# One hybrid decoder layer on one core: a norm row spread by products, a separate bank for the first sums, early small tables, and one query copy moved to VectorE

## The chip, the core and the metric

The kernel runs on one core of a Trainium2 chip. A core has TensorE (PE: matrix products; its weight loads are shown as PEld), VectorE (DVE), ScalarE (ACT), GpSimd (POOL) and SyncE (SP, which here only issues transfers), a two-dimensional on-chip memory of 128 rows, and a smaller accumulation memory of eight banks into which TensorE writes. Transfers between the chip's main memory and the on-chip memory are run by 16 DMA engines. They are issued from SP, ACT and POOL. The engines run side by side and wait for each other by semaphores; each takes its own instructions in the order of the program.

The metric is the device time of one execution in microseconds (us).

## The reference, cut to what matters

One layer is computed twice: for a prompt of 1024 tokens (8 tiles of 128) and for a sample step of 8 sequences of 8 tokens with 512 cached tokens each. Both begin with a root-mean-square norm and one combined projection of 3872 columns.

```python
def rms_norm(x, g):
    x32 = x.astype(jnp.float32)
    y = x32 * lax.rsqrt(jnp.mean(x32 * x32, axis=-1, keepdims=True) + EPS)
    return (y * g.astype(jnp.float32)).astype(x.dtype)
...
    h = rms_norm(x, g_norm)
    proj = jnp.einsum('btd,dn->btn', h, w_in)
    qa, kc, vc, ks, vs, kw, vw, ga, za, qb, kb, vb, fb, zb = jnp.split(proj, SPLIT_POINTS, axis=-1)
...
    # group A: sparse attention, three branches with gates
    return gates[..., 0:1] * o_c + gates[..., 1:2] * o_s + gates[..., 2:3] * o_w
    # group B (fox): softmax attention with a decaying bias
    s = s + (jnp.transpose(cq, (0, 2, 1))[:, :, :, None] - jnp.transpose(ck, (0, 2, 1))[:, :, None, :])
...
    u = jnp.concatenate([oa.reshape(B, T, -1) * jax.nn.silu(za), ob.reshape(B, T, -1) * jax.nn.silu(zb)], axis=-1)
    return x + jnp.einsum('btm,md->btd', u, w_out).astype(x.dtype)
```

At these sizes the prompt has 16 selection blocks and the reference takes the 16 best, so the selected branch is plain causal attention.

## The kernel before, in words

**Stages.** The projection runs over 15 chunks of at most 288 columns; chunk 0 holds keys and values of the compressed branch. Each chunk goes over 8 prompt tiles and one tile of sample tokens. Eleven chunks run first, with the cache's compression as background work; the last four are mixed with the attention of group B. Then comes the attention of group A, one tile of 128 queries after the other (`nsa_tile`), mixed in tiles 0 to 3 with the sample's attention (`sample_nsa`, `sample_fox`) and from tile 4 on with the output projection (`project_out`, and `project_last` for the last tile).

**Number format.** A float32 operand is split into a high and a low float16 part, and a product is three products: high by high, high by low, low by high. So a tile of x gives `xth` and `xtl`, a chunk of weights gives `wsp` with both parts, and attention probabilities give `phi` and `plo`.

**The start.** `first_loads` fetches the norm's weights g twice: as `g8`, 8 numbers to a row, from which a product with `ones` and a reduction make the common scale `gmax`, and as `gb`, the whole row of 1024 in each of the 128 rows, written by one broadcast transfer. `x_tile(0)` squares a tile on ScalarE (L163), makes its scale on POOL (L164, L165), multiplies x by scale and `gb` on VectorE (L166, tile `xsq`), turns it on TensorE (L171) and splits it on ScalarE (L176, `xth`) and VectorE (L177, `xtl`). `load_w` fetches a chunk's weights in four quarters (`wst`), squares them on ScalarE (L202), sums the squares with a product with `ones` (L205), reduces on VectorE (L206, L207), takes the power -0.5 on POOL (L208), and then scales and splits (L220, L216, L217 on ScalarE; L221 on VectorE; L218 on POOL). The products of the projection are L246. The sums of L205 and the transposes of L171 share the two banks named `tr`.

**Late in the program.** `nsa_queries(t)` fetches, scales and splits the queries of tile t, turns them on TensorE (L1076) and copies the result to `q1` on ScalarE (L1080); a transfer issued by ScalarE (L1081) copies its rows 64 to 127 to rows 0 to 63 of `qm` (`nqm` in the profile). The maxima of the scores (`nsa_max`, products L1103) need `qm`, and so do the scores (L1147).

**What sets the order.** The program is built with a scheduler that replays the written code against its own model of times and so fixes, engine by engine, the order in which the instructions stand. A change in one place can move instructions in places that it doesn't touch.

Of the kernel before, what the change touches and what calls it, by code (L numbers as in the profile page):

```python
# [11 lines left out]
F32 = mybir.dt.float32  # L12
# [4 lines left out]
AF = mybir.ActivationFunctionType  # L17
# [4 lines left out]
D = 1024  # L22
# [71 lines left out]
def layer_kernel(ctx, tc, a, o):  # L94
    nc = tc.nc
    P = ctx.enter_context(tc.tile_pool(name="const", bufs=1))
# [9 lines left out]
    ones = P.tile([128, 128], F32, name="ones")  # L106
    nhalf = P.tile([128, 32], F32, name="nhalf")
    block = P.tile([24, 512], F16, name="block")
    ident16 = P.tile([128, 128], F16, name="ident16")
    nsc = P.tile([128, 10], F32, name="nsc")  # L110
    wsc = P.tile([128, 16], F32, name="wsc")
    nc.vector.memset(nhalf, -0.5)
# [65 lines left out]

    bank = {"tr": ("ctr", 1), "acc": ("acc", 4, 288), "ws": 2}
    w_in = a["w_in"][0].rearrange("(kt p) n -> p kt n", p=128)  # L180

    def load_w(cols, vcols=None, vi=None, split=None):

# [10 lines left out]
        for q in range(4):  # L194
# [8 lines left out]
            st.append(s)  # L203
        p = PS.tile([128, 12], F32, name="tr", bufs=bank["ws"])
        nc.tensor.matmul(p[:, 0:used], ones, sv[:, 0:used], start=True, stop=True)  # L205
        nc.vector.tensor_reduce(out=sv[:, 12:13], in_=p[:, 0:used], axis=AX.X, op=ALU.add)  # L206
        nc.vector.tensor_scalar(sv[:, 13:14], sv[:, 12:13], 2.0 ** -30, TINY, op0=ALU.mult, op1=ALU.add)  # L207
# [668 lines left out]

    def load_chunk(ci):
        kind, cols, c = chunks[ci]
        vi = {"slc": 0, "win": 1, "vb": 2 + c}.get(kind)
        return load_w(cols, None if vi is None else slice(128, 256) if vi < 2 else slice(0, 256), vi,  # L880
                      True if kind == "z" else None)

# [32 lines left out]
    def first_loads():  # L915
        nc.scalar.dma_start(g8[:, 0], a["g_norm"][0].rearrange("(p k) -> p k", k=8))
        nc.scalar.dma_start(ident, a["c_ident"])
        nc.scalar.dma_start(gb, a["g_norm"].to_broadcast([128, D]))
        nc.vector.memset(ones, 1.0)
        nc.vector.tensor_tensor(g8[:, 1], g8[:, 0], g8[:, 0], op=ALU.mult)  # L920
        p = PS.tile([128, 512], F32, name="tr", bufs=2)
        nc.tensor.matmul(p[:, 0:8], ones, g8[:, 1], start=True, stop=True)
        nc.vector.tensor_reduce(out=gmax[:, 1:2], in_=p[:, 0:8], axis=AX.X, op=ALU.add)
        nc.vector.tensor_scalar(gmax[:, 0:1], gmax[:, 1:2], 2.0 ** -30, 1e-30, op0=ALU.mult, op1=ALU.max)
        nc.vector.tensor_scalar(gmax[:, 3:4], gmax[:, 0:1], D * EPS, None, op0=ALU.mult)

    def setup():
# [4 lines left out]
    def setup_loads():  # L932
        for i, n in enumerate(("gq_a", "gk_slc", "gk_win", "gq_b", "gk_b", "gk_cmp")):
            nc.sync.dma_start(grow[:, 64 * i:64 * i + 64], a[n])
        nc.sync.dma_start(grow[:, 384:392], a["b_f"])
        nc.sync.dma_start(block, a["c_block"])
        nc.sync.dma_start(ptab, a["page_table"].rearrange("(one b) j -> one (b j)", one=1))

# [11 lines left out]
    x_tile(0)  # L950
    setup()
    loaded = load_chunk(0)
    x_tile(1)
# [17 lines left out]
    PS = SP.enter_context(tc.tile_pool(name="ps2", bufs=1, space=PSUM, reuse_waits="tile"))  # L971
    bank.update({"smax": ("smax", 2), "tr": ("tr", 1), "acc": ("acc", 2, 512), "pv": ("pv", 1), "ws": 1})
    C2 = SC.enter_context(tc.tile_pool(name="fxc", bufs=1, reuse_waits="tile"))
# [93 lines left out]
    def nsa_queries(t):  # L1067
        q = BN.tile([128, 8, 64], F32, name="nq", bufs=1)
        nc.sync.dma_start(q.rearrange("p h d -> p (h d)"), qpark[t])
        qsp = BN.tile([128, 8, 128], F16, name="nqs", bufs=1)  # L1070
        split16(q, nsc[:, 1:2], qsp[:, :, 64:128], qsp[:, :, 0:64], nc.gpsimd if t else nc.vector)
        r = []
        for g in range(2):
            p = turned(t)
            for i in range(4):
                nc.tensor.transpose(p[:, i * 128:(i + 1) * 128], qsp[:, 4 * g + i], ident16)  # L1076
            q1 = BN.tile([128, 512], F16, name="nq1", bufs=4)
            qm = BN.tile([128, 512], F16, name="nqm", bufs=4)
            nc.gpsimd.memset(qm[64:88], 0.0)
            nc.scalar.activation(q1, p, AF.Copy)  # L1080
            nc.scalar.dma_start(qm[0:64], q1[64:128])  # L1081
            r.append((q1, qm))
        return r
# [136 lines left out]
    nc.gpsimd.dma_start(cnew, a["c_new"])  # L1220
    heado = C5.tile([128, 2], F32, name="heado")
    nc.sync.dma_start(heado, a["c_head"])
    spread = C5.tile([128, NB, 128], F32R, name="spread")
# [26 lines left out]
    def sample_decay():  # L1250
# [3 lines left out]
        l8 = B5.tile([64, NB, 8], F32, name="sl8", bufs=1)  # L1254
        bm = B5.tile([64, 8], F32, name="sbm", bufs=1)
        nc.sync.dma_start(bm, a["c_batch"][0:64])
        nc.vector.tensor_tensor(l8, bc(logf[0:64, 8:9], [64, NB, 8]), bc(bm[:, :, None], [64, NB, 8]), op=ALU.mult)
# [397 lines left out]
```

## Time and profile before

| | |
|---|---|
| three runs (us) | 973.31, 966.92, 971.30; median 971.3 |
| the profiled execution (us) | 971.47, of which the span of the core is 969.7 |
| granted TensorE clock, mean over the span | 0.979 |
| busy share of the span | PE 93%, PEld 70%, DVE 67%, ACT 66%, POOL 38% |

A row of the time line reads: start, duration, engine, line of the code, operation, what it writes and reads, shape, number; in brackets the idle time of that engine ahead of it and what ended it. TensorE's products are pipelined and their shown durations overlap; the distance of two starts is what one costs. The granted clock is a share of TensorE's full speed: 1.00 is 2.4 GHz and 0.50 is 1.2 GHz.

### The profile page before, as it was taken

How to read it: one execution, taken by the hardware profiler on the slowest of the kernel's cores; microseconds unless marked ns; L12 is line 12 of the kernel's file. 1: busy time of each engine (PE TensorE's matmuls, PEld its weight loads, DVE VectorE, ACT ScalarE, POOL GpSimd, SP SyncE). 2: the span in 40 equal slices, each digit the busy share in tenths (PEclk: the TensorE clock that was granted, in tenths of full speed). 3: DMA queues.
4: the chain of work that ended last, by engine and by line, in shares of the span. 5: the costliest groups of instructions: out<-in, count | busy, mean ns of one | idle time of the engine just before them, and what ended most of it. 6: DMA issues, size and time to landing. Idle time of an engine off the chain costs nothing. (4 is left out here: it accounts for less than half of the span.)

```text
span 969.7 us, 24710 instructions
## 1 busy us (share of the span) xinstructions
PE 901.2 (93%) x9099; PEld 679.7 (70%) x9099; DVE 652.5 (67%) x1894; ACT 642.3 (66%) x1379; POOL 368.0 (38%) x548
## 2 busy tenths in 40 slices
PE   4899999999999999999999888889999989999997
PEld 3688799788887888877777566566666656555554
DVE  5764665564555425687887666797978796778755
ACT  6754643443456554987886688887988966557662
POOL 4535657755677441361522311343321312101211
PEclk9899999999999999999999799999999999999999
DMA  7563324332345342354452755755455323213221
GB/s 267 141 151 110 85 67 116 99 98 82 94 142 198 97 115 84 91 164 151 152 169 70 221 166 157 231 161 183 153 172 196 91 66 99 96 56 88 92 94 66
DMA packets 125756, 124.32 MB, mean 128 GB/s; under 512 B 39404, under 2 KB 103572, under 8 KB 125612
## 3 DMA queue, kind: packets, MB, share of 16 engines
q1 hardware_dynamic: 120900, 119.07, 40.2%
q10 hardware_dynamic: 4048, 2.43, 1.0%
q0 software_dynamic: 688, 1.25, 0.6%
q8 instruction: 71, 1.16, 0.5%
q14 instruction: 49, 0.40, 0.1%
HBM read 87.96 MB, written 31.61 MB: 123 GB/s over the span
## 5 line engine op out<-in xcount | busy, mean ns | idle before, releaser
L246 PE MATMUL acc<-wsp,xth 128*128 128x256 f16 (+1 forms) x1920 | 337.4, 277 | 5.7 <-ACT xth L176 2.8
L246 PE MATMUL acc<-wsp,xtl 128*128 128x256 f16 (+1 forms) x960 | 265.4, 277 | 0.0
L246 PEld LDWEIGHTS <-xth 128*128 128x128 f16 x1920 | 188.5, 99 | 35.5 <-issue 3.3
L1152 ACT ACTIVATE pf<-st,nsc 128x512 f32<-128x512 f32 x132 | 98.7, 780 | 22.4 <-PE st L1148 13.1
L246 PEld LDWEIGHTS <-xtl 128*128 128x128 f16 x960 | 95.1, 99 | 14.8 <-issue 1.4
L729 PEld LDWEIGHTS <-phi 128*128 128x128 f16 x816 | 77.4, 97 | 15.2 <-ACT phi L719 3.3
L731 PEld LDWEIGHTS <-plo 128*128 128x128 f16 x816 | 77.2, 100 | 9.5 <-DVE plo L1155 2.6
L1153 ACT ACTIVATE phi<-pf 128x1024 f16<-128x1024 f32 (+1 forms) x76 | 71.3, 948 | 18.5 <-PE pv L731 15.1
L730 PEld LDWEIGHTS <-phi 128*128 128x128 f16 x816 | 77.2, 98 | 5.7 <-issue 0.6
L1155 DVE TENSOR_TENSOR plo<-pf,phi 128x1024 f16<-128x1024 f32 (+1 forms) x58 | 64.8, 1123 | 13.8 <-ACT phi L1153 13.3
L265 POOL TENSOR_TENSOR nss<-nss,nhalf 128x4 f32<-128x4 f32 (+3 forms) x72 | 68.8, 956 | 4.4
L716 ACT ACTIVATE pf<-st,nsc 128x512 f32<-128x512 f32 (+1 forms) x96 | 63.0, 673 | 9.4 <-PE st L782 4.7
L1155 POOL TENSOR_TENSOR plo<-pf,phi 128x1024 f16<-128x1024 f32 (+1 forms) x18 | 36.7, 2040 | 78.7 <-ACT phi L1153 66.5
L202 ACT ACTIVATE vsq<-wst 128x512 f16<-128x512 f32 (+2 forms) x72 | 40.1, 558 | 31.5 <-DMA wst<-in_w_in_dram 31.1
L729 PE MATMUL pv<-va,phi 128*128 128x65 f16 x528 | 58.5, 193 | 2.6 <-DVE nt L1132 1.7
L730 PE MATMUL pv<-va,phi 128*128 128x64 f16 x528 | 58.3, 195 | 0.0
L731 PE MATMUL pv<-va,plo 128*128 128x65 f16 x528 | 56.1, 192 | 1.6 <-DVE plo L1155 1.1
L1103 PE MATMUL smax<-kma,nqm 88*128 88x512 f16 (+3 forms) x192 | 49.9, 317 | 4.4 <-DMA nqm<-nq 2.0
L1147 PE MATMUL st<-nqm,kma 88*128 88x512 f16 x132 | 50.3, 381 | 2.3 <-ACT pf L1152 1.9
L719 ACT ACTIVATE phi<-pf 128x512 f16<-128x512 f32 (+1 forms) x96 | 48.8, 526 | 5.3 <-PE pv L731 5.0
L721 DVE TENSOR_TENSOR plo<-pf,phi 128x512 f16<-128x512 f32 (+3 forms) x77 | 46.9, 617 | 7.0 <-ACT phi L719 4.8
L749 DVE CUSTOM_DVE_ANT_0 junk<-smax,maskw,nm 128x512 bf16<-128x512 f32 x64 | 47.6, 743 | 4.4 <-PE smax L1103 2.9
(465 smaller groups left out, 2351.1 us busy)
## 6 DMA issues: line engine op xcount, KB each, us to landing
wst<-in_w_in_dram SPq DMA_DIRECT2D x56, 256.0 KB
sfk<-in_cache_fox_kv_dram SPq DMA_DIRECT2D x32, 256.0 KB
sfv<-in_cache_fox_kv_dram SPq DMA_DIRECT2D x32, 256.0 KB
out_dram<-kv SPq DMA_DIRECT2D x52, 128.0 KB
xin<-in_x_prompt_dram SPq DMA_DIRECT2D x8, 512.0 KB
cpair<-in_cache_nsa_cmp_kv_dram SPq DMA_DIRECT2D x64, 64.0 KB
xin<-in_w_out_dram SPq DMA_DIRECT2D x8, 512.0 KB
zpark<-z SPq DMA_DIRECT2D x32, 128.0 KB
```

Of the source, the lines that this page charges most:

```text
L246: nc.tensor.matmul(ps[:, :n], x[:, k, t * 128:(t + 1) * 128], w[k // 2][:, i, k % 2, :n], start=(k == 0 and j == 0), stop=(k == KT - 1 and ...
L265: nc.gpsimd.tensor_tensor(ss[:n, 0, :h], ss[:n, 1, :h], nhalf[:n, :h], op=ALU.pow)
L716: nc.scalar.activation(p[:n, :cols], ps[:n, :cols], AF.Exp, bias=nsc[:n, 3:4], scale=nsc[:n, 6:7])
L719: nc.scalar.activation(hi[:n, :cols], p[:n, :cols], AF.Copy)
L729: nc.tensor.matmul(po[:, s, 0:65], hi[:, c], v[:, 0:65], start=f, stop=False, skip_group_check=True)
L730: nc.tensor.matmul(po[:, s, 0:64], hi[:, c], v[:, 65:129], start=False, stop=False, skip_group_check=True)
L731: nc.tensor.matmul(po[:, s, 0:65], lo[:, c], v[:, 0:65], start=False, stop=l, skip_group_check=True)
L1103: nc.tensor.matmul(pr[:, r], qm[0:88, (r0 + r) * 128:(r0 + r + 1) * 128], kma[0:88, 2 * k + g, j0 * 128:j1 * 128], start=r == 0, stop=not ...
L1147: nc.tensor.matmul(ps, kma[0:88, 2 * k + g, c], qm[0:88], start=True, stop=False)
L1152: nc.scalar.activation(pf[:, 512 * x:512 * x + 512], ps, AF.Exp, bias=nsc[:, 3:4], scale=nsc[:, 2:3])
L1153: nc.scalar.activation(hi[:, 0:n], pf[:, 0:n], AF.Copy)
L1155: (nc.gpsimd if turn[0] % share[mixed[0]] == 0 else nc.vector).tensor_sub(lo_[:, 0:n], pf[:, 0:n], hi[:, 0:n])
```

## The change

Four edits. The broadcast transfer of `gb` becomes a transfer of the one row; two products of that row with the first row of `ones` write it to all 128 rows of two `acc` banks, and VectorE and ScalarE copy one half each. The sums of the first chunk's weights get a bank of their own (`sa`) in place of a `tr` bank, and the instructions of `setup()` are issued behind those sums' product. The two small tables `heado` and `sbm` move from the sample's buffers to buffers that last, and are fetched at the start. For tile 1 of the queries, VectorE copies rows 64 to 127 of the turned queries out of the accumulation bank to rows 0 to 63 of `qm`, in place of the transfer.

```diff
-    bank = {"tr": ("ctr", 1), "acc": ("acc", 4, 288), "ws": 2}
+    bank = {"tr": ("ctr", 1), "acc": ("acc", 4, 288), "ws": 1, "sum": "sa"}
...
-    def load_w(cols, vcols=None, vi=None, split=None):
+    def load_w(cols, vcols=None, vi=None, split=None, first=None):
...
-        p = PS.tile([128, 12], F32, name="tr", bufs=bank["ws"])
+        p = PS.tile([128, 12], F32, name=bank["sum"], bufs=bank["ws"])
         nc.tensor.matmul(p[:, 0:used], ones, sv[:, 0:used], start=True, stop=True)
+        if first is not None:
+            first()
...
         nc.scalar.dma_start(g8[:, 0], a["g_norm"][0].rearrange("(p k) -> p k", k=8))
+        nc.scalar.dma_start(gb[0:1], a["g_norm"])
         nc.scalar.dma_start(ident, a["c_ident"])
-        nc.scalar.dma_start(gb, a["g_norm"].to_broadcast([128, D]))
...
         nc.vector.tensor_scalar(gmax[:, 3:4], gmax[:, 0:1], D * EPS, None, op0=ALU.mult)
+        for h in range(2):
+            c = slice(512 * h, 512 * h + 512)
+            p = PS.tile([128, 512], F32, name="acc", bufs=4)
+            nc.tensor.matmul(p, ones[0:1], gb[0:1, c], start=True, stop=True)
+            if h:
+                nc.scalar.activation(gb[:, c], p, AF.Copy)
+            else:
+                nc.vector.tensor_copy(gb[:, c], p)
...
         nc.sync.dma_start(block, a["c_block"])
+        nc.sync.dma_start(heado, a["c_head"])
+        nc.sync.dma_start(bm, a["c_batch"][0:64])
...
-    setup()
-    loaded = load_chunk(0)
+    loaded = load_chunk(0, setup)
+    bank.update({"sum": "tr", "ws": 2})
...
-            nc.scalar.dma_start(qm[0:64], q1[64:128])
+            if t == 1:
+                nc.vector.tensor_copy(qm[0:64], p[64:128])
+            else:
+                nc.scalar.dma_start(qm[0:64], q1[64:128])
...
-    heado = C5.tile([128, 2], F32, name="heado")
-    nc.sync.dma_start(heado, a["c_head"])
...
-        bm = B5.tile([64, 8], F32, name="sbm", bufs=1)
-        nc.sync.dma_start(bm, a["c_batch"][0:64])
```

The order that the scheduler makes differs from the one before in two stretches: at the start, up to about the 940th of TensorE's 15,757 instructions, and from the sample's first transposes to the end, about the last 7,000. Between them it is the same. Three places follow. Line numbers in the changed kernel are 2 to 17 higher: L166 is there L168, L206 is L210, L925 is L929, L1080 is L1094, L1597 is L1610.

VectorE at the start, before:

```order
L920 TENSOR_TENSOR g_105<-g_105 128x8
L923 TENSOR_REDUCE gmax<-tr 128x1
L924 TENSOR_SCALAR gmax<-gmax 128x1
L925 TENSOR_SCALAR gmax<-gmax 128x1
L930 RECIPROCAL gmax<-gmax 128x1
L166 SCALAR_TENSOR_TENSOR xsq<-xin,xst,gb 128x1024
L177 TENSOR_TENSOR xtl<-tr,xth 128x4x128
```

VectorE at the start, in the changed kernel:

```order
L924 TENSOR_TENSOR g_107<-g_107 128x8
L937 COPY gb<-acc 128x512
L927 TENSOR_REDUCE gmax<-tr 128x1
L928 TENSOR_SCALAR gmax<-gmax 128x1
L210 TENSOR_REDUCE vst<-sa 128x1
L929 TENSOR_SCALAR gmax<-gmax 128x1
L211 TENSOR_SCALAR vst<-vst 128x1
L942 RECIPROCAL gmax<-gmax 128x1
L213 RECIPROCAL vst<-vst 128x1
L214 TENSOR_SCALAR un<-vst,gmax 128x1
L168 SCALAR_TENSOR_TENSOR xsq<-xin,xst,gb 128x1024
```

The reduction of the first weights' sums (L210) now stands ahead of L929, whose result the scale of x's first tile needs, and the first tile's multiplication (L168) stands behind the weights' chain instead of ahead of it.

ScalarE at the queries of tile 1, before (`nq` is the copy `q1`, `nqm` is `qm`; the other rows belong to group B and to the sample):

```order
L1080 ACTIVATE nq_10522<-smax 128x512
L1403 ACTIVATE ot_9362<-ctr 64x8x8
L716 ACTIVATE pf<-st,nsc 128x512
L1065 DMA kma<-k1a 64x4x128
L719 ACTIVATE phi<-pf 128x512
L1081 DMA nqm<-nq_10522 64x512
```

ScalarE and, in the second fence, VectorE at the queries of tile 1, in the changed kernel:

```order
L1094 ACTIVATE nq_10528<-smax 128x512
L1094 ACTIVATE nq_10538<-smax 128x512
L1064 ACTIVATE nqs<-nq 128x8x64
L1305 ACTIVATE spt<-ctr 128x512
L723 ACTIVATE phi<-pf 128x128
```

```order
L1297 RECIPROCAL sms<-sms 128x1
L1308 COPY spt<-ctr 128x128
L1096 COPY nqm<-smax 64x512 x2
L1129 TENSOR_REDUCE nm<-smax 128x2
L725 TENSOR_TENSOR plo<-pf,phi 128x128
```

Both groups' queries of tile 1 are now copied one right after the other, on ScalarE to `q1` and on VectorE to `qm`, and the reductions of their maxima (L1129) follow.

TensorE at the end, before (`pv` is the last product of the last tile's attention, `ctr<-woh,uh` the second of three parts of its output projection, `st<-woh,uh` the third):

```order
L731 MATMUL pv<-va_66,plo 128x65
L1589 MATMUL ctr<-ident,z 128x128
L1597 LDWEIGHTS uh
L1597 MATMUL ctr<-woh,uh 128x512
L1597 LDWEIGHTS uh
L1597 MATMUL ctr<-wol,uh 128x512
```

TensorE at the end, in the changed kernel:

```order
L734 MATMUL pv<-va_68,phi 128x64
L735 LDWEIGHTS plo
L735 MATMUL pv<-va_68,plo 128x65
L1602 MATMUL ctr<-ident,z 128x128 x2
L1610 LDWEIGHTS uh
L1610 MATMUL st<-woh,uh 128x512
```

The 12 products of the second part stood between the last attention product and the last transposes; now they stand ahead of the last attention products, and only the third part's 12 are left behind them.

## Rows read from the trace of the kernel before

**Rows 1.** Stages: us, PE, PEld, DVE, ACT, POOL busy, clock, DMA share, GB/s.

```profile
0.00:75.00 75.00, 55.76 (x419) 46.47 (x420) 48.45 (x145) 48.60 (x130) 34.62 (x68) 0.95 0.63 182
560.00:800.00 240.00, 217.93 (x2714) 149.07 (x2713) 192.36 (x550) 201.39 (x407) 67.67 (x86) 0.98 0.50 156
800.00:950.00 150.00, 148.62 (x1326) 84.98 (x1325) 105.91 (x232) 94.42 (x132) 27.75 (x36) 0.99 0.27 88
950.00:969.70 19.70, 13.88 (x113) 6.81 (x111) 10.79 (x19) 4.84 (x10) 1.75 (x3) 1.00 0.16 55
```

**Rows 2.** Time line of the start, 4 to 24 us, all engines.

```profile
4.90 0.59 PE L922 MATMUL tr<-g,ones 128*128 128x8 f32 x2 [4.90 <-DVE g L920]
...
7.16 0.56 POOL L165 TENSOR_TENSOR xst<-xst,nhalf 128x1 f32<-128x1 f32 x1
...
9.62 1.28 DVE L166 SCALAR_TENSOR_TENSOR xsq<-xin,xst,gb 128x1024 f32<-128x1024 f32 x1 [2.23 <-DMA gb<-in_g_norm_dram]
...
10.67 0.63 ACT L202 ACTIVATE vsq<-wst 128x512 f16<-128x512 f32 x1
...
10.96 1.97 PE L171 MATMUL tr<-ident,xsq 128*128 128x128 f32 x8 [5.47 <-DVE xsq L166]
...
14.26 0.59 PE L205 MATMUL tr<-vst,ones 128*128 128x4 f32 x2 [1.34 <-DVE xtl L177]
...
16.34 1.64 POOL L208 TENSOR_TENSOR vst<-vst,nhalf 128x1 f32<-128x1 f32 x1
...
18.01 0.72 ACT L220 ACTIVATE wsp<-wst,vst 128x512 f16<-128x512 f32 x1 [2.94 <-POOL vst L208]
...
18.78 0.37 PE L246 MATMUL acc<-wsp,xth 128*128 128x256 f16 x1 [0.75 <-ACT wsp L220]
...
23.83 0.96 PE L246 MATMUL acc<-wsp,xth 128*128 128x256 f16 x5
```

**Rows 3.** Time line of TensorE, 28 to 78 us.

```profile
28.78 1.04 PE L171 MATMUL tr<-ident,xsq 128*128 128x128 f32 x8
...
38.37 0.60 PE L246 MATMUL acc<-wsp,xth 128*128 128x256 f16 x2 [2.83 <-ACT xth L176]
...
46.73 0.63 PE L171 MATMUL tr<-ident,xsq 128*128 128x128 f32 x4 [1.12 <-DVE xtl L177]
...
50.35 0.92 PE L942 MATMUL tr<-grow,ones 1*128 1x392 f32 x2
```

**Rows 4.** Windows of the start, columns as in rows 1.

```profile
5.00:10.00 5.00, 0.49 (x2) 0.40 (x2) 1.02 (x5) 2.31 (x9) 1.64 (x4) 1.00 0.98 324
...
35.00:40.00 5.00, 1.96 (x11) 1.22 (x10) 3.50 (x13) 4.11 (x8) 3.51 (x7) 0.80 0.56 138
40.00:45.00 5.00, 5.00 (x26) 3.82 (x25) 3.39 (x3) 4.53 (x13) 2.11 (x4) 0.52 0.67 153
45.00:50.00 5.00, 3.88 (x36) 3.34 (x35) 3.64 (x7) 4.13 (x18) 1.34 (x3) 1.00 0.49 129
```

**Rows 5.** Time line at the queries of tile 1.

```profile
591.64 0.47 ACTq L1081 DMA_DIRECT2D nqm<-nq  x1
...
597.59 0.47 PE L1103 MATMUL smax<-kma,nqm 88*128 88x256 f16 x2 [1.98 <-DMA nqm<-nq]
```

**Rows 6.** Windows of the same place, columns as in rows 1.

```profile
596.00:597.00 1.00, 0.00 (x0) 0.00 (x0) 0.00 (x0) 1.00 (x3) 0.65 (x1) 1.00 0.89 283
...
600.00:601.00 1.00, 1.00 (x6) 0.71 (x5) 0.59 (x1) 1.00 (x3) 0.25 (x1) 0.50 0.00 0
```

**Rows 7.** L1268 of VectorE: count, duration in ns (min/median/max), starts, forms.

```profile
L1268 DVE SCALAR_TENSOR_TENSOR ch<-ctr,ch x2: 218/450/683, 555.5 to 557.2; 64x512 fp32r<-64x512 f32 x1, 64x64 fp32r<-64x64 f32 x1
```

**Rows 8.** Windows around the sample's end, columns as in rows 1.

```profile
790.00:800.00 10.00, 5.87 (x33) 3.58 (x31) 8.73 (x30) 4.41 (x7) 2.21 (x5) 0.79 0.26 79
800.00:820.00 20.00, 20.00 (x205) 12.87 (x204) 12.94 (x24) 12.09 (x18) 3.30 (x5) 0.94 0.25 77
```

**Rows 9.** The chain that ended last, its last products: start, us, what.

```profile
963.15 2.78 PE st L1597 x12
```

More of the change, by code (lines that the diff above doesn't have):

```diff
@@ L110, in layer_kernel @@
     nsc = P.tile([128, 10], F32, name="nsc")
+    heado = P.tile([128, 2], F32, name="heado")
+    bm = P.tile([64, 8], F32, name="sbm")
     wsc = P.tile([128, 16], F32, name="wsc")
@@ L875, in layer_kernel, with load_chunk @@
     win_rows = a["cache_nsa_win_kv"][0].rearrange("b t s g d -> b t (s g d)")
-    def load_chunk(ci):
+    def load_chunk(ci, first=None):
         kind, cols, c = chunks[ci]
@@ L880, in load_chunk @@
         return load_w(cols, None if vi is None else slice(128, 256) if vi < 2 else slice(0, 256), vi,
-                      True if kind == "z" else None)
+                      True if kind == "z" else None, first)
     def project_chunk(ci, tab, wn):
@@ L971, in layer_kernel @@
     PS = SP.enter_context(tc.tile_pool(name="ps2", bufs=1, space=PSUM, reuse_waits="tile"))
-    bank.update({"smax": ("smax", 2), "tr": ("tr", 1), "acc": ("acc", 2, 512), "pv": ("pv", 1), "ws": 1})
+    bank.update({"smax": ("smax", 2), "tr": ("tr", 1), "acc": ("acc", 2, 512), "pv": ("pv", 1), "ws": 1, "sum": "tr"})
     C2 = SC.enter_context(tc.tile_pool(name="fxc", bufs=1, reuse_waits="tile"))
```

## The prediction

> **What bounds the kernel now.** I read the stages first [rows 1]. TensorE is busy for 148.6 of 150 us from 800 on and for nearly all of the middle, so time is to be had only where it waits: 19.2 us in the first 75, 22.1 us between 560 and 800, and 5.8 us in the tail. Next I read what it waits for in those stretches, and the granted clock behind each wait, because a wait can cost twice here. After the 2.83 us wait that ends at 38.37 [rows 3] the clock falls to 0.50: 0.80 and 0.52 as means of two windows of 5 us [rows 4] make 2 x (0.20 + 0.48) x 5 = 6.8 us at 1.2 GHz, and half of that, 3.4 us, is lost on top. After the 1.98 us wait for a query copy [rows 5] it is 1.00 while TensorE stands still, and 0.50 from 598 to 601 (its last us: [rows 6]). After the wait at the sample's end it is 0.79 over 10 us, with 4.13 us idle, and 0.94 over the next 20 [rows 8]. The shorter wait of 1.12 us at 46.73 [rows 3] leaves the clock at 1.00 [rows 4].
>
> The Trainium skill, "TensorE: Matmul & The Clock Gate" (Part 1: The HAM clock gate), says that throttled is the default state and that only activity releases it. [...]
>
> **The start.** Before, the first tile's multiplication waits 2.23 us for the broadcast row and starts at 9.62. The weights are squared by 11.3 (10.67 + 0.63), but their sums' product starts only at 14.26, when VectorE frees a bank, and POOL's power behind it takes 1.64 us beside a VectorE multiplication, against 0.56 for the same kind of instruction at 7.16. So ScalarE gets the scale at 18.01 and the first projection product starts at 18.78 [rows 2].
>
> In the changed kernel 508 KB less are moved while the DMA engines are 98% busy at 324 GB/s [rows 4]: 1.6 us. So I put the last quarter's squares at 9.1 to 9.9, the accumulator's read included. The two new products: 392 columns in float32 took 0.92 us [rows 3], so 512 take 1.2 at full speed. At the start TensorE runs at half pace (eight transposes in 1.97 us [rows 2], later in 1.04 [rows 3]), so 2.4 each, 4.8 for both. They can start when the row is there, about when `g8` is (4.90 [rows 2]), and end at 9.7. The product for `gmax`, 0.59 us, stands behind them in the queue and ends at 10.3; the sums' product, as long, ends at 10.9.
>
> Here the order costs something: VectorE now does the reduction of the weights' sums ahead of the number that the first tile's scale needs. That scale, which POOL had finished at 7.7 before, now waits for the weights. Three small VectorE steps (some 0.5 us in all) and four POOL steps of at most 0.56 us follow, the weights' power third: weights' scale at 13.1, first tile's multiplication from 13.6 to 14.9. ScalarE then has six weight instructions of about 0.7 us, 4.2 in all, ahead of the first `xth`: first projection product at about 17.9, 0.9 us earlier than 18.78. But before, the second tile's eight transposes had been done by then; now they follow, and cost 1.04 to 1.97 us. I take 0 for the start; its bounds are -2.5 (the weights' scale at 13.1 instead of 18.01 lets the later tiles through sooner) and +2.
>
> The wait at 38.37 comes as ScalarE does the second chunk's weights ahead of the fifth tile's `xth`. In the new order half of that tile's `xth` stands ahead of those weights: 12 products more to do, which at the full pace of this stretch (five starts between 23.83 and 24.6 [rows 2], about 0.11 us apart) last 1.3 us. I take -1.3 and leave the clock's loss where it is; the bounds are 0 and -6.2 (2.83 + 3.4).
>
> The copies of the spread row out of the banks (one each on VectorE and ScalarE) are hidden behind the wait for the weights' landing. If that lands sooner they cost at most one such copy, 0.7 us.
>
> **The small tables.** Two transfers less stand in SP's queue ahead of the sample's pages, two more at the start ahead of the second chunk's weights, whose buffers are free no earlier than the first chunk's splits. Nobody waits for either table in the trace. I take 0, with bounds of +-0.5. What moves is the order behind it.
>
> **The queries of tile 1.** The transfer was issued at 591.64 and its reader started at 597.59 [rows 5]: 5.95 us, of which TensorE stood idle for 1.98. Neither TensorE nor VectorE did anything between 596 and 597 [rows 6], so two copies on VectorE have room. Their price: VectorE's L1268 reads rows 0 to 63 of a bank and writes rows 64 to 127, 64x512, in 0.68 us [rows 7]; two are 1.4 us in place of 5.95. Behind them on VectorE stand the reductions of the same maxima, which need them anyway. The wait goes, 1.98, and with it 3 us at half speed, 1.5: -3.5. Bounds: 0 (the next operand is late) and -3.5.
>
> The Trainium skill's "VectorE: DVE Perf Modes" (Why tensor_reduce can't reduce along partition axis) says that each of the 128 lanes is a pipeline of its own with no path across. By that the copy by 64 rows could not replace the transfer, this term would be 0 and the forecast 970.9. The row of L1268 shows such a move, so the row decides.
>
> **The sample's end.** Idle time 4.13 us, and 2 x (0.21 x 10 + 0.06 x 20) = 6.6 us at half speed [rows 8], some 2 of them idle, so 2.3 lost: 6.4 together. TensorE waited there for VectorE, with the output projection's first transposes stuck in its queue ahead of attention products. In the new order 60 attention products stand ahead of those transposes. I take half, -3.2; bounds 0 and -6.4.
>
> **The tail.** The last products of the second part, 12 of them, lay in the shadow of the chain from the last attention product through VectorE, ScalarE and POOL to the third part. Now they stand ahead of it. In a stretch that is bound by TensorE [rows 1] this moves the end by 12 products, 2.78 us for as many of the same shape [rows 9]: +2.8. Bounds: 0 (if TensorE would have waited for the last probabilities anyway) and +2.8.
>
> **Everything else that is rearranged** in the 400 us from the sample's start: the same work in another order, with 22.1 us of waits between 560 and 800, of which the two above are 6.1. I allow for one new wait of the common size, 1.12 us as at 46.73, which leaves the clock alone: +1.1. Bounds -4 and +6 (one new wait of the size of the sample's end).
>
> **The sum**, against the profiled execution's 971.47 (its span 969.7 and 1.8 outside; the median of the three runs is 971.3, so nothing is to be corrected): 0 - 1.3 + 0 - 3.5 - 3.2 + 2.8 + 1.1 = -4.1, 967.4 us.
>
> **Rivals.** *The long waits go, and with them their clock.* The start's wait is worth 6.2, the copy 3.5, the sample's end 6.4, and the tail gives back 2.8: -13.3, 958.2. For it: three waits account for all of this, and each stands next to something that moved. Against it: two of the three only get some more work in front of them.
>
> *Only the copy works.* The wait at 597.59 goes, the others stay, and the tail and one new wait take the rest: -3.5 + 2.8 + 1.1 = +0.4, 971.9. For it: most of the change touches nothing that TensorE waits for.
>
> *The first tile is held by the weights, and it ends slower.* VectorE's queue puts the weights' sums ahead of the first tile's scale. If the weights land no earlier than before (10.67), sums, scale and first multiplication come 1.6 us later than in my chain, and the eight transposes are owed as well: +2 at the start. The tiles then come late enough that a second wait of about 2 us with its half-speed stretch appears, +3.5, while the copy's gain is spent on the next operand; with the tail's 2.8 that is +8.3 less the 3.2 at the sample's end: 976.6. It decides from the point where the last quarter lands after about 10.5 us.
>
> **How the numbers follow.** One per cent, 9.7 us, is about what a measurement of this kernel can tell from no change; its three runs lie 6.4 us apart. Chances: the forecast (963 to 970) 0.52, all long waits 0.18, only the copy 0.18, slower 0.12. Faster by over 1% (below 961.6) is the second case and the forecast's lower edge, 0.20; slower by over 1% (above 981.0) is the far end of the last, 0.03. The range 958.5 to 976 leaves out the lower half of the second case and the upper half of the last.
>
> **What would show it.** First projection product between 16.5 and 19; a float32 product pair of 512 columns at 2 to 2.5 us each before 10; VectorE idle ahead of L210 while L929 could run; no DMA named as what ended a wait of L1120 at tile 1, and no window of 0.50 there; a shorter wait at the sample's end; and some 12 us from the last attention product to the end with TensorE idle for 2.8 us more. The prediction is wrong if the reordered stretch has two or more new waits of 2 us, each with its half-speed stretch, or loses two of the old ones beyond those named.

## The result and the profile after

The changed kernel takes 966.17 us (median of 20 runs) against 971.53 for the kernel before: ratio 0.9943, 95% interval 0.9921 to 0.9965. Runs over 1.5% above the fastest of their kernel are left out of the ratios and means. The profiled execution took 964.45 us, its span 962.7, its granted clock 0.983.

The stages of the changed kernel, columns as in [rows 1]:

```profile
0.00:75.00 75.00, 60.02 (x438) 47.65 (x438) 50.96 (x150) 49.13 (x131) 37.70 (x72) 0.98 0.62 181
560.00:800.00 240.00, 221.71 (x2701) 148.32 (x2700) 191.50 (x555) 196.89 (x397) 66.50 (x86) 0.99 0.48 151
800.00:950.00 150.00, 146.44 (x1354) 83.37 (x1350) 106.15 (x231) 94.29 (x132) 25.02 (x33) 1.00 0.27 87
950.00:962.70 12.70, 4.78 (x14) 1.66 (x14) 3.63 (x9) 1.40 (x4) 0.74 (x2) 0.80 0.11 41
```

TensorE is busy for 4.3 us more in the first 75 and for 3.8 us more between 560 and 800 than in [rows 1]. Of the 4.3, 3.75 are the row's two products themselves (first row below), so this is no gain. Behind 950 the clock is 0.80.

The start, from the time line of all engines (compare [rows 2]; L207 is the sums' product, L210 their reduction, L250 the projection):

```profile
4.49 3.75 PE L933 MATMUL acc<-gb,ones 1*128 1x512 f32 x4 [4.49 <-DMA gb<-in_g_norm_dram]
...
7.96 0.63 ACT L204 ACTIVATE vsq<-wst 128x512 f16<-128x512 f32 x1
...
8.73 0.59 PE L207 MATMUL sa<-vst,ones 128*128 128x4 f32 x2
...
9.36 0.16 DVE L210 TENSOR_REDUCE vst<-sa 128x1 f32<-128x4 f32 x1 [0.20 <-PE sa L207]
9.44 0.14 DVE L929 TENSOR_SCALAR gmax<-gmax 128x1 f32<-128x1 f32 x1
...
10.61 0.55 POOL L212 TENSOR_TENSOR vst<-vst,nhalf 128x1 f32<-128x1 f32 x1
...
11.20 0.72 ACT L224 ACTIVATE wsp<-wst,vst 128x512 f16<-128x512 f32 x1 [1.00 <-POOL vst L212]
...
15.33 0.61 PE L250 MATMUL acc<-wsp,xth 128*128 128x256 f16 x2 [0.28 <-ACT xth L178]
```

The last quarter of the weights is squared 2.7 us earlier, the power on POOL takes 0.55 instead of 1.64, and the first projection product starts at 15.33 instead of 18.78 (17.88 in a second profile of the kernel before).

VectorE and TensorE at the next long wait, in the place of the one at 38.37 in [rows 3]:

```profile
38.33 2.17 DVE L168 SCALAR_TENSOR_TENSOR xsq<-xin,xst,gb 128x1024 f32<-128x1024 f32 x1 [1.42 <-POOL xst L167]
40.42 1.64 DVE L225 SCALAR_TENSOR_TENSOR wsp<-wst,vst,wsp 128x512 f16<-128x512 f32 x1
...
42.18 0.68 DVE L179 TENSOR_TENSOR xtl<-tr,xth 128x512 f16<-128x512 f32 x1
...
43.00 1.09 PE L173 MATMUL tr<-ident,xsq 128*128 128x128 f32 x4 [3.90 <-DVE xtl L179]
```

Here much of the lead is lost again: 3.90 us, because a tile's low part stands behind the next tile's multiplication and the second chunk's weights.

The queries of tile 1 and what follows, first the two VectorE copies (duration in ns, starts, forms), then the first maxima (L1120), the next wait of TensorE and windows around it, columns as above:

```profile
L1096 DVE COPY nqm<-smax x2: 419/422/425, 588.4 to 588.7; 64x512 f16<-64x512 f16 x2
```

```profile
589.47 0.38 PE L1120 MATMUL smax<-kma,nqm 88*128 88x256 f16 x2
...
591.83 0.56 POOL L1481 DMA_DIRECT2D stairt<-in_c_stairt_dram  x1
...
598.21 0.38 PE L1187 MATMUL st<-stairt,identb 128*128 128x512 bf16 x1 [3.16 <-DMA stairt<-in_c_stairt_dram]
```

```profile
595.00:598.20 3.20, 0.05 (x1) 0.00 (x0) 0.00 (x0) 1.89 (x5) 0.00 (x0) 1.00 0.93 243
598.20:602.00 3.80, 3.79 (x31) 1.78 (x31) 2.21 (x4) 2.44 (x6) 0.72 (x1) 0.64 0.59 164
602.00:605.00 3.00, 3.00 (x42) 2.37 (x40) 1.56 (x9) 2.42 (x7) 0.52 (x1) 0.89 1.01 293
770.00:790.00 20.00, 17.96 (x171) 10.31 (x168) 19.77 (x43) 14.46 (x21) 4.98 (x6) 1.00 0.22 67
790.00:810.00 20.00, 18.76 (x168) 10.67 (x166) 13.57 (x38) 12.44 (x18) 2.83 (x6) 1.00 0.36 116
```

The maxima of tile 1 wait for no transfer. But 10 us later TensorE stands still for 3.16 us, for a constant table (`stairt`, the staircase of the compressed branch), and runs slowly behind it. In the kernel before the same transfer, issued at 606.0, lands 4.2 us later, just ahead of its reader at 610.29. The sample's end (the last two rows; compare [rows 8]) has lost its half-speed stretch.

The tail, from the chain that ended last (start, us, what):

```profile
949.59 0.04 PE pv L735
...
952.96 0.52 ACT z L1529
...
953.52 0.45 PE ctr L1602 x2
...
954.44 4.35 PE st L1610 x12
```

TensorE's wait for the last transposes, in the changed kernel and, in the second fence, before:

```profile
953.52 0.44 PE L1602 MATMUL ctr<-ident,z 128*128 128x128 f32 x2 [3.91 <-ACT z L1529]
```

```profile
962.24 0.44 PE L1589 MATMUL ctr<-ident,z 128*128 128x128 f32 x2 [0.73 <-ACT z L1516]
```

The same 12 products that took 2.78 us in [rows 9] take 4.35 here, behind a wait of 3.91 us in place of 0.73.

### The profile page after: what moved, and what is told of

The parts are those of the page before. It is cut to its first block, busy times and chain, and to the rows that moved or that the text cites. A ratio compares the mean times of both kernels' runs of the same rounds, so it can differ in the third digit from the quotient of the medians.

```text
span 962.7 us, 24720 instructions
## 1 busy us (share of the span) xinstructions
PE 900.2 (94%) x9103; PEld 676.5 (70%) x9103; DVE 649.4 (67%) x1897; ACT 641.7 (67%) x1380; POOL 365.4 (38%) x548
## 4 chain that ended last, share of the span: by engine, by line
PE 60%; DMA 11%; DVE 9%; ACT 7%; issue 4%; POOL 3%; SPq 2%; ACTq 0%; POOLq 0%; DVEq 0%
PE acc L250 20%; PE ctr L1572 7%; PE sa L479 4%; DMA sfk<-in_cache_fox_kv_dram 3%; PE acc L243 2%; PE smax L1120 2%; PE st L1164 2%; DMA wst<-in_w_in_dram 2%; PE st L1165 2%; PE pv L735 2%; PE pv L733 2%; PE pv L734 2%; DVE junk L753 1%; PE ctr L1379 1%; DMA xin<-in_w_out_dram 1%
## 5 line engine op out<-in xcount | busy, mean ns | idle before, releaser
L250 PE MATMUL acc<-wsp,xth 128*128 128x256 f16 (+1 forms) x1920 | 335.6, 276 | 1.8 <-DVE z L412 0.8
L250 PE MATMUL acc<-wsp,xtl 128*128 128x256 f16 (+1 forms) x960 | 264.6, 276 | 0.1
L250 PEld LDWEIGHTS <-xth 128*128 128x128 f16 x1920 | 187.7, 99 | 30.7 <-issue 1.5
L250 PEld LDWEIGHTS <-xtl 128*128 128x128 f16 x960 | 94.6, 99 | 15.1 <-issue 1.5
L1172 DVE TENSOR_TENSOR plo<-pf,phi 128x1024 f16<-128x1024 f32 (+1 forms) x58 | 62.5, 1082 | 8.0 <-ACT phi L1170 7.1
L1172 POOL TENSOR_TENSOR plo<-pf,phi 128x1024 f16<-128x1024 f32 (+1 forms) x18 | 34.5, 1917 | 49.6 <-ACT phi L1170 37.6
L1165 PE MATMUL st<-nq,k1a 128*128 128x512 f16 x132 | 50.1, 379 | 0.0
## 6 DMA issues: line engine op xcount, KB each, us to landing
out_dram<-kv SPq DMA_DIRECT2D x52, 128.0 KB
zpark<-z SPq DMA_DIRECT2D x32, 128.0 KB
```

Source lines behind the costliest of these rows:

```text
L250: nc.tensor.matmul(ps[:, :n], x[:, k, t * 128:(t + 1) * 128], w[k // 2][:, i, k % 2, :n], start=(k == 0 and j == 0), stop=(k == KT - 1 and ...
L1165: nc.tensor.matmul(ps, k1a[:, 2 * k + g, c], q1, start=False, stop=not (diag or far))
L1172: (nc.gpsimd if turn[0] % share[mixed[0]] == 0 else nc.vector).tensor_sub(lo_[:, 0:n], pf[:, 0:n], hi[:, 0:n])
```

## The experiments

To place a difference I cut each profiled execution at two instructions that both orders contain: stage A ends at the ScalarE row that starts at 127.98 in the profile before, stage B at the one at 538.34, stage C with the span. TensorE's order in B is the same in all kernels here. All times in us; ratios of the runs to those of the kernel before in the same comparison, with 95% intervals.

| kernel | ratio (interval) | A | B | C | span |
|---|---|---|---|---|---|
| before | | 128.0 | 410.4 | 431.4 | 969.7 |
| before again (e8) | | 127.5 | 407.9 | 431.8 | 967.1 |
| changed | 0.9943 (0.9921 to 0.9965) | 127.4 | 405.0 | 430.3 | 962.7 |
| changed again (e3) | 0.9939 (0.9912 to 0.9966) | 126.5 | 410.0 | 431.1 | 967.5 |
| copy alone (e1) | 0.9997 (0.9965 to 1.0029) | 125.1 | 404.6 | 434.2 | 963.8 |
| row alone (e9) | 1.0000 (0.9970 to 1.0031) | 128.8 | 404.7 | 433.3 | 966.7 |
| sums' bank alone (e10) | 1.0038 (1.0014 to 1.0062) | 129.4 | 409.7 | 428.8 | 967.9 |
| both edits of the start (e4) | 0.9973 (0.9942 to 1.0004) | 128.6 | 406.0 | 432.2 | 966.8 |
| tables and copy, no start (e12) | 1.0055 (1.0026 to 1.0084) | 127.0 | 408.9 | 438.5 | 974.4 |
| changed without the row (e2) | 1.0030 (1.0001 to 1.0059) | 131.6 | 410.5 | 432.1 | 974.2 |
| changed, staircase early (e5) | 0.9936 (0.9910 to 0.9963) | 126.0 | 411.4 | 427.8 | 965.2 |
| changed, tail (e6) | 0.9936 (0.9907 to 0.9965) | 125.3 | 408.2 | 425.7 | 959.2 |
| staircase and tail (e7) | 0.9932 (0.9907 to 0.9956) | 127.2 | 406.6 | 424.5 | 958.2 |
| e7, second chunk later (e11) | 0.9930 (0.9895 to 0.9965) | 124.0 | 406.0 | 426.1 | 956.0 |

Column B is the first finding: 404.6 to 411.4 in fourteen executions with one order. So 5.4 of the 7.0 us by which the two first profiles differ stand in a stage in which TensorE's order is unchanged, and lie inside this scatter: that the change gains anything there is not shown.

**e3 and e8: the same two kernels again.** No edit.

> The changed kernel once more, for a second profile of it. Theory A and its rival say nothing of the middle, whose order is that of before. If the middle's 5.4 us (405.0 against 410.4 from landmark to landmark) are chance of one profiled execution, this profile shows 405 to 411 there and half-speed stretches at other places. If they are a consequence of the earlier start, it shows 405 to 406 again and the same stretches. Total: ratio 0.992 to 0.9965.

> The kernel before once more, for a second profile of it. Theory C (its middle was slow by chance in the first profile): from 128 to 538 us it takes 404 to 408 here instead of 410.4, with other stretches at 1.2 GHz. Its rival (the start of the kernel before costs the middle 5 us each time): 409 to 411 again. Sample's end: waits of 2.0 and 1.8 us and two stretches at 1.2 GHz again.

Both came out as chance would have it: the changed kernel's B was 410.0 this time, that of the kernel before 407.9. The faster median came again (0.9939). By stages, though, the means of the two profiles of each kernel differ by 0.8 us in A, 1.6 in B and 0.9 in C, against 5.4 between the medians of the first comparison.

**e1: the copy alone.**

```diff
+            if t == 1:
+                nc.vector.tensor_copy(qm[0:64], p[64:128])
+            else:
+                nc.scalar.dma_start(qm[0:64], q1[64:128])
```

> The kernel before with one part of the change: VectorE copies the queries of tile 1; start and tables as before. TensorE's order differs from the kernel before by 56 instructions around the copy and nowhere else. Theory A (the copy's wait is what it gains): no transfer ends a wait of the first maxima of tile 1, the stretch from 560 to 800 is 2.0 to 3.5 us shorter, ratio 0.9964 to 0.998. Theory B (the next operand is as late): another wait of 1 to 3 us stands within 10 us of that place, total within 1 us of before. Theory C (the gain of the change came out of the unchanged middle by chance): the copy does nothing of its own, and the time from 128 to 538 us, 410.4 in the profile of before, comes out anywhere from 405 to 411.

Time line of TensorE at the maxima of tile 1 in this kernel, and a window behind it:

```profile
587.29 0.33 PE L1369 MATMUL ctr<-ident,sfk 128*128 128x128 f32 x1 [1.44 <-DMA sfk<-in_cache_fox_kv_dram]
588.91 0.58 PE L1106 MATMUL smax<-kma,nqm 88*128 88x256 f16 x2 [1.22 <-DMA kma<-k1a]
```

```profile
589.00:590.00 1.00, 1.00 (x9) 0.81 (x9) 0.26 (x1) 0.00 (x0) 0.00 (x0) 0.50 0.26 78
```

Theory B. The transfer of the queries is gone, and the same product now waits for that of the *keys* of tile 1 (`kma<-k1a`, issued by ScalarE at 581.69), besides a page of the sample's cache. The two waits are 2.66 us together; the kernel before has 0.57 for the page and the 1.98 of [rows 5], 2.55. Half speed follows here too. Ratio 0.9997: the copy by itself is worth nothing that this can measure (3.5 us less would be 0.9964, just outside the interval).

**e9, e10, e4: the edits of the start, each and both.** e9 has the row's products alone, e10 the bank and the moved `setup()` alone, e4 both; tables and copy as before.

For e9:

```diff
-        nc.scalar.dma_start(gb, a["g_norm"].to_broadcast([128, D]))
...
+            nc.tensor.matmul(p, ones[0:1], gb[0:1, c], start=True, stop=True)
```

For e10:

```diff
-    bank = {"tr": ("ctr", 1), "acc": ("acc", 4, 288), "ws": 2}
+    bank = {"tr": ("ctr", 1), "acc": ("acc", 4, 288), "ws": 1, "sum": "sa"}
...
-    setup()
-    loaded = load_chunk(0)
+    loaded = load_chunk(0, setup)
```

> The kernel before with the two edits of the start (row by products, first sums in a bank of their own), without the early tables and without the copy. The order of TensorE is that of the changed kernel at the start, that of before in the middle, in the tail and most of the last 400 us; 2,000 instructions of the sample's first part are rearranged. Theory A: start 0 to -1.3, the waits for the copied queries and at the sample's end are there again, and the tail is 2.8 to 4 us shorter than the changed kernel's: total -1 to -3, ratio 0.997 to 0.999. Rival (the start and its shifted phase are all of it): ratio 0.993 to 0.995.

> The kernel before with the row by products alone (first sums in a tr bank, tables and copy as before). TensorE's order differs at the start and in 2,000 instructions of the sample's first part, as in the run with both edits of the start. Theory A (the row's products are the part that pays; the bank of its own adds nothing): first projection product at 15 to 17, mean time 2 to 3 us under before, ratio 0.997 to 0.998. Rival (only the two edits together pay): ratio 0.999 to 1.001.

> The kernel before with the first sums in a bank of their own and setup behind their product, and the norm row by the broadcast transfer. Behind the start, TensorE's order is that of before but for 24 instructions. Theory A (without the row's products this order is worse, as the changed kernel without them was 3.6 us slower than before in the mean): a wait of 4 us or more ahead of the first page transposes near 80, ratio 1.002 to 1.005. Rival (that wait was chance): ratio 0.998 to 1.001.

The first projection product in e9 and, in the second fence, in e10, then the wait of TensorE near 80 in e10:

```profile
18.00 0.37 PE L246 MATMUL acc<-wsp,xth 128*128 128x256 f16 x1
```

```profile
15.10 0.61 PE L248 MATMUL acc<-wsp,xth 128*128 128x256 f16 x2 [1.72 <-ACT xth L176]
...
78.24 0.66 PE L469 MATMUL ctr<-ident,cpair 128*128 128x128 f32 x4 [2.37 <-ACT cx L471]
```

The row alone: nothing (its rival was right), and the first product comes at 18.00, where theory A had 15 to 17. It is the bank that brings it forward: 15.10 with the broadcast row. Yet the bank alone is 0.38% slower, as theory A said, but not by the wait that it named: 2.37 us at 78, not 4, and the two profiles of the kernel before have 2.14 and 3.15 there. What makes it slower stays open. Both together: 0.9973, theory A's ratio, with an interval that touches 1 and also the rival's 0.995. So neither edit pays alone, and an earlier first product is not by itself a gain.

**e2: the changed kernel without the row's products.**

```diff
+        nc.scalar.dma_start(gb, a["g_norm"].to_broadcast([128, D]))
...
-            nc.tensor.matmul(p, ones[0:1], gb[0:1, c], start=True, stop=True)
```

> The changed kernel with the norm row by the broadcast transfer again; everything behind the first 530 instructions of TensorE stands in the same order as in the changed kernel. Theory A (the start is worth what the sum said, 0 to 1.3): first projection product at 16.5 to 18.8 instead of 15.33, and at the 128th us 0 to 1.3 later than the changed kernel: total +0 to +1.3, ratio to before 0.9943 to 0.9957. Rival (the start's 3.45 us are kept to the end): total +3.4, ratio 0.998. Theory C (chance in the middle): the 405.0 us from there to the sample come out longer, without anything changed there.

TensorE in this kernel near 80, and the windows there:

```profile
79.91 1.12 PE L471 MATMUL ctr<-ident,cpair 128*128 128x128 f32 x4 [5.43 <-ACT cx L473]
```

```profile
76.00:80.00 4.00, 0.09 (x1) 0.09 (x2) 0.00 (x0) 1.41 (x6) 0.00 (x0) 0.79 0.76 208
80.00:85.00 5.00, 5.00 (x23) 5.00 (x24) 2.96 (x12) 4.11 (x15) 1.91 (x4) 0.50 0.52 164
```

Theory A and its rival both expected too little: ratio 1.0030 where 0.998 was the rival's. Nor is the first projection product late, as theory A had it: it comes at 15.08. The interval (1.0001 to 1.0059) does not overlap with that of the changed kernel in the same comparison (0.9912 to 0.9966), so with the other edits in place the row's products are worth some 0.9%. Stage A is 4 to 5 us longer, C (432.1, same order) hardly. In this one profile the place is a wait of 5.43 us near 80 with half speed behind it; there ScalarE has the squares of a chunk's weights, which have not landed, ahead of the copy that TensorE needs. In e10, with the same bank, that wait is 2.37, so one long wait of one execution is no account of the 0.9%.

**e12: tables and copy without the start.** The kernel before with these two edits.

```diff
+    heado = P.tile([128, 2], F32, name="heado")
+    bm = P.tile([64, 8], F32, name="sbm")
...
+                nc.vector.tensor_copy(qm[0:64], p[64:128])
```

> The kernel before with the early tables and the copy, start as before: TensorE's order is that of the changed kernel from the sample's first transposes up to its 12,893rd instruction, and differs in the last 2,600. Theory A (the rearranged sample gives at its end what the staircase table takes back, the stages from 538 on being 431.6 before and 431.2 after): ratio 0.998 to 1.001. Rival (the start's 2.1 us are the smaller half, the rest comes from here): ratio 0.996 to 0.998.

Windows of its tail, and the wait there:

```profile
950.00:952.00 2.00, 1.20 (x27) 1.11 (x28) 2.00 (x2) 1.72 (x4) 0.00 (x0) 1.00 0.00 0
952.00:956.00 4.00, 4.00 (x31) 2.26 (x30) 2.59 (x5) 3.58 (x6) 2.13 (x1) 0.57 0.02 4
962.00:965.00 3.00, 0.00 (x0) 0.00 (x0) 1.34 (x5) 0.82 (x3) 0.74 (x2) 0.56 0.00 0
965.00:970.00 5.00, 4.27 (x13) 1.69 (x14) 0.83 (x3) 0.58 (x2) 0.00 (x0) 0.58 0.00 0
```

```profile
965.25 0.69 PE L1592 MATMUL ctr<-ident,z 128*128 128x128 f32 x2 [3.90 <-ACT z L1519]
```

Neither theory: 0.55% *slower*, and stage C takes 438.5 instead of 431.2. Up to TensorE's 12,893rd instruction the sample's order is that of the changed kernel; the last 2,600 stand otherwise, and there TensorE has two half-speed stretches in the last 25 us where the changed kernel has one. With both edits of the start (-0.27%) this adds up to +0.28%; the whole change measures -0.57%. The parts don't add; each set of edits gets its own order from the scheduler, down to the tail.

**e5, e6, e7: what the changed kernel still loses.** e5 keeps the staircase table in a lasting buffer and issues its transfer earlier; e6 queues the 12 products of the second part behind the last attention product; e7 has both.

For e5:

```diff
+    stairt = P.tile([128, T], BF16, name="stairt")
...
+    tc.keep_in_program_order(nc.gpsimd.dma_start(stairt, a["c_stairt"]))
...
-    stairt = B3.tile([128, T], BF16, name="stairt")
-    nc.gpsimd.dma_start(stairt, a["c_stairt"])
```

For e6:

```diff
+            final[0] = nc.tensor.matmul(po[:, s, 0:65], lo[:, c], v[:, 0:65], start=False, stop=l, skip_group_check=True)
...
+                with tc.issue_after(final[0].ins) if ks.start == 0 else ExitStack():
```

> The changed kernel with the staircase table in a buffer that lasts, so that its transfer is issued about 16 us earlier; on TensorE 4 instructions near its first reader change places, nothing else. In both profiles of the changed kernel TensorE waits about 3 us for that transfer (3.16 and 3.03) and then runs 3.4 us at 1.2 GHz. Theory A (this wait took the place of the copy's, and can be taken out by itself): no wait of over 1 us between 595 and 602, 540 to the end is 3.0 to 4.9 us shorter, ratio to before 0.989 to 0.991. Rival (as with the copy alone, the next operand is as late): another wait of 2 to 3 us within 10 us, ratio 0.993 to 0.996.

> The changed kernel with the 12 products of the second part of the last output projection put behind the last attention product, as they stood before; the rest of TensorE's order is unchanged. Theory A (the tail gave back what the sum said and more): the wait of 3.91 us ahead of the last transposes falls to 0.7 to 1.3, the last 12 products run at full speed (2.78 instead of 4.35 us), and the kernel ends 2.6 + 1.6 = 4.2 us earlier, ratio to before 0.989 to 0.991. Rival (the last attention products wait for their probabilities anyway): a new wait stands ahead of them, only the 1.6 us of speed come back, ratio 0.992 to 0.993.

> The changed kernel with both edits, the early staircase table and the 12 products behind the last attention product. Theory A: the two gains add, 7 to 9 us under the changed kernel, ratio to before 0.985 to 0.988. Rival (the next operands are late): 0.990 to 0.993.

e5 at the place of the wait:

```profile
595.00:602.00 7.00, 6.99 (x67) 4.89 (x66) 4.89 (x14) 6.94 (x18) 1.89 (x3) 1.00 0.48 133
```

e6 in its last 16 us, TensorE's waits, then the end of its chain:

```profile
944.27 0.20 PE L737 MATMUL pv<-va,plo 128*128 128x65 f16 x1 [1.49 <-DVE plo L1174]
951.64 0.44 PE L1604 MATMUL ctr<-ident,z 128*128 128x128 f32 x2 [1.93 <-ACT z L1531]
```

```profile
952.55 2.78 PE st L1613 x12
```

In the profiles both go the way theory A says. In e5 TensorE is busy for 6.99 of the 7 us, and stage C is 3.4 us under the mean of the three executions with the changed order (430.3, 431.1, 432.1). In e6 the 12 products are back at 2.78 us, the wait at the end falls from 3.91 to 1.93 (not to the 0.7 to 1.3 of theory A), and C is 5.5 shorter, in spite of a new wait of 1.49 ahead of the last attention products, which was the rival's. e7 has C at 424.5. The timed runs show less: 0.9936, 0.9936 and 0.9932, outside theory A's ranges each time, so e5 to e7 can't be told from the changed kernel by their ratios. By the medians they are 4.3, 6.9 and 8.2 us under before in their comparison.

**e11: e7 with the second chunk's weights loaded one tile later.**

```diff
-            if t == 1:
+            if t == (1 if ci else 2):
                 loaded = load_chunk(ci + 1)
```

> The changed kernel with the early staircase table and the 12 products behind the last attention product, and the second chunk's weights loaded and split one tile later. It is meant for the wait of 3.9 us at 43, where VectorE's low parts of those weights (1.64 us) stand ahead of the low part of a tile that TensorE waits for. Theory A: that wait falls to 2 us or less with at most one stretch at 1.2 GHz behind it, 2 to 4 us under the run with stair and tail alone, ratio to before 0.988 to 0.991. Rival (the second chunk's products then wait for their weights as long): ratio 0.991 to 0.994.

TensorE's waits in it between 38 and 48, and a window between them:

```profile
40.88 0.39 PE L251 MATMUL acc<-wsp,xth 128*128 128x256 f16 x2 [2.03 <-ACT xth L179]
47.44 0.92 PE L959 MATMUL tr<-grow,ones 1*128 1x392 f32 x2 [1.68 <-DVE xtl L180]
```

```profile
41.00:45.00 4.00, 3.42 (x29) 2.69 (x28) 2.68 (x4) 4.00 (x10) 2.92 (x6) 1.00 0.70 158
```

The wait of 3.9 us becomes two, 2.03 and 1.68, with the clock at 1.00 behind the first, and stage A is the shortest of all, 124.0. Ratio 0.9930: that is in the rival's range (0.991 to 0.994), not in theory A's. The median, 959.96, is the lowest here, but 8.0 us under before in its comparison where e7 has 8.2, so no gain over e7 is shown. It beats the kernel before beyond its interval. That it beats the changed kernel is likely by the medians (5.4 and 4.5 us under before in its two comparisons) and not shown by the ratios.

**Waiting or clock?** Each run lists its span and its mean granted clock; span times clock is the time at full speed, work and waits together, and the rest is what half speed cost. Means over the runs, in us, each beside those of the kernel before in the same comparison:

| kernel | at full speed | before | lost to half speed | before |
|---|---|---|---|---|
| copy alone (e1) | 949.8 | 949.3 | 17.0 | 17.5 |
| row alone (e9) | 948.9 | 949.4 | 17.7 | 16.9 |
| sums' bank alone (e10) | 949.8 | 949.4 | 18.9 | 16.9 |
| tables and copy, no start (e12) | 953.0 | 949.4 | 18.0 | 16.9 |
| changed without the row (e2) | 951.5 | 949.3 | 18.9 | 17.5 |
| both edits of the start (e4) | 944.8 | 949.3 | 19.9 | 17.5 |
| changed again (e3) | 945.3 | 949.3 | 16.8 | 17.5 |
| changed, staircase early (e5) | 945.5 | 950.6 | 17.2 | 17.7 |
| changed, tail (e6) | 945.1 | 950.6 | 16.8 | 17.7 |
| staircase and tail (e7) | 945.0 | 950.6 | 15.5 | 17.7 |
| e7, second chunk later (e11) | 945.3 | 949.4 | 13.6 | 16.9 |

The six kernels with both edits of the start need 944.8 to 945.5 us at full speed, all others 948.9 to 953.0; the standard errors of these means are 0.4 to 1.0. So the change takes out about 4 us of waits, and they come with the row's products and the sums' bank together; neither has them alone. With the start in place, copy and tables add nothing to this (945.3 against 944.8). What they and the later edits move is the loss to half speed: 19.9 with the start alone, 16.8 in the changed kernel in the same comparison (18.3 in the first), 13.6 in e11. Where in the kernel the 4 us lie the stages can't say, since B alone scatters by 6.8, and why it takes both edits stays open.

## Why the forecast was right, and by which steps

967.4 was forecast, 966.17 measured; -4.1 against -5.4 us between the medians. The sign and the size were right. Of the single terms several were not, and that they made up for each other is luck.

**The start** (0, bounds -2.5 to +2): first product at 15.33, forecast 17.9 (and its sign, 16.5 to 19, missed). The weights landed a microsecond earlier than I had put them and the two row products took 3.75 us together instead of 4.8, so the sums' product ends at 9.3 instead of 10.9; the steps behind it took a microsecond less as well. Stage A is 0.8 us shorter (means of two profiles each), inside the bounds. But for the whole execution the term is mis-sized: both edits of the start take out 4.5 us at full speed and give back 2.4 in clock (e4), and I had looked for their worth in the first 40 us alone. The step that I feared, L210 ahead of L929, cost little: L210 starts at 9.36 after a wait of 0.20 us for the sums, L929 at 9.44. The slower rival hung on weights that land after 10.5; they were squared by 8.6.

**The wait at 38** (-1.3, bounds 0 and -6.2): wrong. I put half a tile of products in front of it and did not follow VectorE's own queue. The wait is 3.90, longer by 1.1, outside the bounds.

**The tables** (0): the transfers were hidden as said. The order that came with them was not free: e12.

**The copy** (-3.5, bounds 0 to -3.5, and +1.1 for a new wait): the step that failed. In e1 its lower bound, "the next operand is late", was the truth: the keys' transfer for the same tile is waited for in its place, and the ratio is 0.9997. In the changed kernel, with another order, neither is waited for, so the -3.5 came. But the staircase table is waited for, 10 us later, for 3.16, and half speed stands behind it (0.64 over 3.8 us and 0.89 over the next 3 make 2 x (0.36 x 3.8 + 0.11 x 3) = 3.4 us at 1.2 GHz, 1.7 lost). I had allowed 1.1 for one new wait; this one is 4.9. I had not asked when the new order issues that table against when it reads it.

**The sample's end** (-3.2): right. 4.13 us idle and a clock of 0.79 over 10 us and 0.94 over 20 [rows 8] became 3.28 us idle in 40 at a clock of 1.00: 0.85 us less idle and the 2.3 of half speed, 3.1 together. The second profiles of both kernels repeat it.

**The tail** (+2.8, its upper bound): mis-sized. The mechanism was right, TensorE stands idle in the shadow that the 12 products had filled: 3.91 instead of 0.73, +3.2. But the clock falls during that wait and the last 12 products cost 1.6 more: +4.8. I had said that a wait can cost twice and then priced this one once. In e6's profile, with the products back in the shadow, they take 2.78 again and the wait is 1.93, so the order is the cause there; the timed runs can't show what that is worth.

So copy and new wait came out at +1.4 where the sum had -2.4, and the tail at +4.8 where it had +2.8. With the sample's end stage C should be 3.1 us longer by these terms; in the profiles it is 0.9 shorter (two each), and no single run here isolates what else in the reordered stretch made that up. The start gave more than the sum had. That the total came within 1.3 us is luck, not the sum of right terms.

## What to carry to other kernels

Where a scheduler orders the program, an edit is timed together with the order that it brings: the copy, the row and the bank alone measure 0, 0 and +0.4%, tables with copy +0.6%, both edits of the start -0.3%, and the whole -0.6%. Before you compare such kernels, split each run into its time at full speed and its loss to half speed; here the first separates the kernels where the ratios leave them together. Before a wait for one operand is bought off, look when the *other* operand of that instruction lands. And work that fills the shadow of the last chain can be worth more than its length: without the 12 products of 2.78 us, the end has 3.2 us more of idle time and 1.6 us of half speed in this profile.

## What the runs showed of the hardware that was not expected

The length of a wait doesn't decide whether half speed follows. In the changed kernel two waits are as good as equal, 1.66 us ending at 587.08 and 1.67 ending at 667.50; TensorE's rows, then the windows ahead of and behind each:

```profile
587.08 0.66 PE L1304 MATMUL ctr<-ident,spr 128*128 128x128 f32 x4 [1.66 <-ACT spr L1294]
...
667.50 1.33 PE L1379 MATMUL ctr<-ident,sfk 128*128 128x128 f32 x5 [1.67 <-DMA sfk<-in_cache_fox_kv_dram]
```

```profile
585.00:587.00 2.00, 0.42 (x12) 0.30 (x9) 0.00 (x0) 0.75 (x3) 0.45 (x1) 1.00 0.90 308
587.00:591.00 4.00, 3.92 (x36) 3.36 (x37) 2.39 (x8) 4.00 (x12) 1.31 (x2) 1.00 0.37 108
665.80:667.50 1.70, 0.03 (x1) 0.00 (x0) 1.63 (x4) 1.68 (x4) 1.63 (x4) 1.00 1.07 356
667.50:671.00 3.50, 3.50 (x41) 3.16 (x42) 0.70 (x2) 1.19 (x2) 0.98 (x1) 0.51 1.06 392
```

The first leaves the clock at 1.00, the second is followed by 0.51. In the first profile of the kernel before, too, a wait of 2.14 us that ends at 79.13 leaves the clock at 1.00, and the shorter one of 1.98 [rows 5] is followed by 0.50. The Trainium skill, "TensorE: Matmul & The Clock Gate" (Part 1: The HAM clock gate), says that how busy TensorE has been of late sets this clock. The trace agrees in so far as every fall named here comes with a wait; what tells the two waits apart it doesn't show. So the same program meets half speed at other places in each execution (between 307 and 312 in the first profile of before, between 77 and 81 in the second, not the other way round). This is part of why stage B scatters: added up over its windows, half speed costs it between 0.0 and 5.1 us in the fourteen executions, and TensorE's idle time in it lies between 11.8 and 17.0.

VectorE moves rows 64 to 127 of a bank to rows 0 to 63 in 0.42 us (L1096 above), where the forecast had 0.68 from [rows 7]. The Trainium skill, "VectorE: DVE Perf Modes" (Why tensor_reduce can't reduce along partition axis), says that each lane is a pipeline of its own with no path across. The trace doesn't agree for a copy whose output starts at another row: it does shift here.
